# First modulation by halves of the features, shift from TensorE columns, context scale put off

## The chip, the core and the metric

The kernel runs on one core of one Trainium2 chip. Its engines run side by side, each through its own queue of instructions in order: TensorE (PE in the rows; PEld is its load of the stationary operand), VectorE (DVE), ScalarE (ACT), GpSimd (POOL) and SyncE (SP), which issues most of the DMAs. They wait for each other at semaphores. The metric is the device time of one execution in microseconds.

## What is computed

A backbone of two layers over 1024 latent tokens of width 1024, with 256 context tokens as a prefix. Each layer takes a root-mean-square norm, a modulation by a learned conditioning vector, a mixer and a mixture of 16 experts. The change is in what stands at the very start of layer 0:

```python
mod = sc_c @ w_mod[l] + b_mod[l]
sh1, scl1, g1, sh2, scl2, g2 = jnp.split(mod[:, None, :], 6, axis=-1)
h = _modulate(_rms(x, norm1[l]), sh1, scl1)        # h * (1 + scale) + shift
if need_c:
    modc = sc_ctx @ w_mod[l] + b_mod[l]
    csh1, cscl1, cg1, csh2, cscl2, cg2 = jnp.split(modc, 6)
    hc = _modulate(_rms(xc, norm1[l]), csh1, cscl1)
...
p = h @ w_in
q, k, v, gb, gc, xs = jnp.split(p, [K_OFF, V_OFF, B_OFF, C_OFF, X_OFF], axis=-1)
...
conv = gb * _short_conv(gc * xs, conv_w)
```

`sc_c` and `sc_ctx` are the conditioning vectors of latent and context after silu. Only the shift and the scale (2 x 1024 of the 6 x 1024 columns of `w_mod[0]`) are wanted before the first product of `h` with a weight. The context's own shift and scale are wanted much later, when the context's `hc` is made for keys and values.

## The kernel before

`layer0_mix` works with features on the partitions: a block of 512 tokens is held as 8 chunks (k = 0 to 7) of 128 features by 512 tokens. Every f32 operand of a product is split into a rounded part (`hi`) and the rest (`lo`), and a product is three matmuls per chunk (lines 385 to 387 in `fmm`): lo weight with hi data, hi with lo, hi with hi. The convolution runs in four groups of 128 channels (`cc`); for each group `conv_products` makes three projections (c, x, b) of both token blocks, that is 2 x 3 x 8 x 3 = 144 matmuls of 512 columns, each into its own bank of PSUM. `conv` then reads the banks (ACT copy in line 399 first).

What comes before the first product: `xn_tile` (four tiles of 128 tokens for block 0, one by one) loads a tile, squares and sums it on ACT, makes the reciprocal root in small steps on DVE (`rsqrt`), scales it on DVE, transposes it with 8 PE transposes (line 350) and copies it out of PSUM on ACT. `first_mods` loads rows of `w_mod` 128 at a time, shift and scale columns together (line 255). The shift is made on PE with the two vectors as the stationary operand and 512 columns of weights moving (line 257), copied to SBUF and turned by eight small transposes (line 279). The scale is accumulated on DVE, elementwise per partition, for latent and context (lines 261 and 263, 1024 wide), and summed over partitions by 16 matmuls of one column (line 269). Lines 283 to 286 add bias and norm for all 8 chunks at once. Then `modulate` makes hi and lo of all chunks: hi on ACT (line 361), lo in two steps (362, 363) on DVE, and for every fourth chunk on POOL.

`conv_weights(0)` loads the first group's three weights and splits them: the cast in line 164 on ACT, the subtraction in line 165 on DVE for c and on POOL for x and b. The tiles of block 1 are normalised between the products of block 0 by `more`. Behind that, `late_mods` accumulates the other modulation vectors on DVE (line 311), one step at a time, driven by `step`.

The code is written in program order; a scheduler with priorities decides in which order instructions stand in each engine's queue, and `mod(0)` is raised with `high_priority(400)`. An engine cannot pass an instruction that waits.

## Time and profile before

| | us |
|---|---|
| median of 3 runs | 2330.22 |
| lowest and highest | 2327.54, 2330.83 |
| profiled execution | 2327.57 |
| its span, first to last instruction | 2325.8 |
| PE busy in the span | 2144.5 (92%) |
| DVE busy | 1908.1 (82%) |
| ACT busy | 1398.4 (60%) |
| POOL busy | 650.5 (28%) |

The busy shares are of the whole span; the two mixtures of experts fill most of it. The change lies in the first 100 us, 4% of the span, so the stage has to be read by itself: which engine waits for which in it, and at what time it hands over to a stretch in which PE has no gaps. A row of the timeline merges equal instructions that follow each other; its first number is the start, the second the time from the first start to the last end. PE's matmuls overlap, so a pace is read from starts. The granted clock is a share of 2.4 GHz; the record has it at 1.00 from the start.

### The profile page before, as it was taken

To read this page: it belongs to the slowest core of one execution; us is meant where nothing else is said; L and a number is where in the kernel's file an instruction comes from. 1 tells how busy PE (TensorE), PEld (TensorE's weight loads), DVE (VectorE), ACT (ScalarE), POOL (GpSimd) and SP (SyncE) were. 2 spreads that over 40 slices of the span, in tenths; PEclk is the share of its full clock that TensorE was granted. 3 is DMA by queue.
4 is the path that set the end of the run, shared out by engine and by line. 5 is a ranking of instruction groups with operands and counts; after the bars stand their busy time and mean duration, and the time that the engine had idled before them with its cause. 6 is when DMAs were issued, how large, how long until landed. Compare 5 with 4: busy or idle time off the path is not lost.

```text
span 2325.8 us, 31653 instructions
## 1 busy us (share of the span) xinstructions
PE 2144.5 (92%) x10568; PEld 1740.9 (75%) x10568; DVE 1908.1 (82%) x2930; ACT 1398.4 (60%) x1864; POOL 650.5 (28%) x501
## 2 busy tenths in 40 slices
PE   7999989999985999999999699999859999999996
PEld 4787758988764788888888577777647888888884
DVE  7744577887498899999999756665989999999997
ACT  4413515777223788887887436233247888888874
POOL 1201101333442243242342220004313343342322
PEclk8999999999997999999999899999979999999998
DMA  8744552222847999999999502746579999999984
GB/s 289 214 118 141 182 203 73 82 73 103 323 173 282 354 363 376 371 369 375 362 370 367 167 28 67 262 165 213 205 277 343 379 369 360 380 374 357 374 316 154
DMA packets 187242, 602.03 MB, mean 259 GB/s; under 512 B 20557, under 2 KB 41790, under 8 KB 184004
## 3 DMA queue, kind: packets, MB, share of 16 engines
q1 hardware_dynamic: 168280, 533.38, 61.8%
q0 software_dynamic: 18800, 66.63, 9.6%
q8 instruction: 85, 1.39, 0.2%
q14 instruction: 77, 0.62, 0.1%
HBM read 545.89 MB, written 54.04 MB: 258 GB/s over the span
## 4 chain that ended last, share of the span: by engine, by line
PE 54%; DVE 17%; DMA 15%; issue 10%; ACT 3%; POOL 1%; SPq 0%; DVEq 0%; POOLq 0%; ACTq 0%
PE psum L1074 27%; DMA buf<-h2buf,buf 9%; DVE buf L165 3%; PE psum L654 3%; PE psum L1056 2%; DMA buf<-in_w_up_dram 2%; PE psum L1277 2%; PE psum L1278 2%; PE psum L1279 2%; PE psum L386 2%; PE psum L387 2%; PE psum L385 2%; PE psum L611 2%; DVE buf L185 2%; PE psum L612 1%
## 5 line engine op out<-in xcount | busy, mean ns | idle before, releaser
L165 DVE TENSOR_TENSOR buf<-buf,buf 128x1024 fp32r<-128x1024 f32 (+1 forms) x862 | 1025.3, 1235 | 87.2 <-ACT buf L164 71.5
L1074 PE MATMUL psum<-buf,buf 128*128 128x512 f32 x4608 | 1075.8, 392 | 2.7 <-ACT buf L1119 2.2
L164 ACT CAST buf<-buf 128x1024 fp32r<-128x1024 f32 (+1 forms) x868 | 876.1, 1020 | 324.4 <-PE psum L1074 153.9
L1074 PEld LDWEIGHTS psum<-buf,buf 128*128 128x128 f32 x4608 | 860.4, 188 | 180.9 <-ACT buf L1119 3.0
L1047 POOL DMA_INDIRECT buf<-h2buf,buf x32 | 230.9, 7215 | 598.2 <-DVE buf L1045 471.1
L386 PE MATMUL psum<-buf,buf 128*128 128x512 f32 (+1 forms) x352 | 135.5, 387 | 4.6 <-POOL buf L363 4.2
L385 PE MATMUL psum<-buf,buf 128*128 128x512 f32 (+1 forms) x352 | 134.1, 386 | 1.5 <-ACT buf L361 1.5
L387 PE MATMUL psum<-buf,buf 128*128 128x512 f32 (+1 forms) x352 | 134.4, 383 | 0.0
L164 ACT CAST buf<-psum 128x512 fp32r<-128x512 f32 (+1 forms) x153 | 88.8, 606 | 73.9 <-PE psum L1056 57.7
L311 DVE SCALAR_TENSOR_TENSOR buf<-buf,buf,buf 128x1024 f32<-128x1024 f32 x80 | 100.2, 1282 | 36.4 <-DMA buf<-in_w_mod_dram 33.5
L165 DVE TENSOR_TENSOR buf<-psum,buf 128x512 fp32r<-128x512 f32 (+1 forms) x153 | 105.2, 709 | 29.4 <-ACT buf L164 25.9
L1120 POOL TENSOR_TENSOR buf<-buf,buf 128x1024 f32<-128x1024 f32 x30 | 75.4, 2513 | 167.2 <-ACT buf L1119 167.2
L619 DVE TENSOR_REDUCE buf<-psum 128x1 f32<-128x1280 f32 x64 | 95.1, 1488 | 30.5 <-PE psum L612 23.4
L822 PE MATMUL psum<-buf,buf 128*128 128x512 f32 (+1 forms) x272 | 105.7, 391 | 0.0
L820 PE MATMUL psum<-buf,buf 128*128 128x512 f32 (+1 forms) x272 | 105.5, 389 | 0.0
L821 PE MATMUL psum<-buf,buf 128*128 128x512 f32 (+1 forms) x272 | 105.2, 388 | 0.0
L1277 PE MATMUL psum<-buf,buf 128*128 128x512 f32 x256 | 103.0, 403 | 1.3 <-DVE buf L165 1.3
L1278 PE MATMUL psum<-buf,buf 128*128 128x512 f32 x256 | 102.1, 399 | 0.0
L1279 PE MATMUL psum<-buf,buf 128*128 128x512 f32 x256 | 101.3, 396 | 0.0
L1056 PE MATMUL psum<-buf,buf 128*128 128x128 f32 x512 | 70.7, 283 | 28.3 <-DMA buf<-h2buf,buf 28.1
L1056 PEld LDWEIGHTS psum<-buf,buf 128*128 128x128 f32 x512 | 61.3, 145 | 40.7 <-DMA buf<-h2buf,buf 34.5
L835 ACT ACTIVATE buf<-buf 128x512 f32<-128x512 f32 (+1 forms) x34 | 20.6, 606 | 114.8 <-DVE buf L834 114.7
(272 smaller groups left out, 2958.5 us busy)
## 6 DMA issues: line engine op xcount, KB each, us to landing
buf<-in_w_gate_dram SPq DMA_DIRECT2D x256, 512.0 KB
buf<-in_w_up_dram SPq DMA_DIRECT2D x256, 512.0 KB
buf<-in_w_down_dram SPq DMA_DIRECT2D x256, 512.0 KB
buf<-in_w_mod_dram SPq DMA_DIRECT2D x80, 512.0 KB
buf<-xbuf SPq DMA_DIRECT2D x24, 512.0 KB
buf<-in_even_w_in_dram SPq DMA_DIRECT2D x20, 512.0 KB
buf<-in_x_dram SPq DMA_DIRECT2D x16, 512.0 KB
buf<-in_w_mod_dram SPq DMA_DIRECT2D x8, 1024.0 KB
```

The lines of the kernel that those rows point to most:

```text
L164: self.nc.scalar.copy(hi, src)
L165: (eng or self.nc.vector).tensor_tensor(out=lo, in0=src, in1=hi.bitcast(F32), op=OP.subtract)
L385: nc.tensor.matmul(out, wl[:, k, :], hh[:, k], start=(k == 0), stop=False)
L386: nc.tensor.matmul(out, wh[:, k, :], hl[:, k], start=False, stop=False)
L387: nc.tensor.matmul(out, wh[:, k, :], hh[:, k], start=False, stop=(k == KC - 1))
L822: nc.tensor.matmul(o, mh[:, k], wl[:, k, cs], start=False, stop=(k == KC - 1))
L1047: gather = nc.gpsimd.indirect_dma_start(out=xg.ap, out_offset=None, in_=self.H2, in_offset=bass.IndirectOffsetOnAxis(ap=idx.ap.bitcast(I32 ...
L1056: nc.tensor.transpose(b[:, j, :], src[:, k * P:(k + 1) * P], self.ident.ap)
L1074: mm = nc.tensor.matmul(self.bank(banks + n), st[:, k % 4], wt[:, n * 512:(n + 1) * 512], start=first, stop=last)
L1277: nc.tensor.matmul(b, hl[:, k], wh[:, k, :], start=(k == 0), stop=False)
L1278: nc.tensor.matmul(b, hh[:, k], wl[:, k, :], start=False, stop=False)
L1279: nc.tensor.matmul(b, hh[:, k], wh[:, k, :], start=False, stop=(k == KC - 1))
```

## The change

`w_mod` is loaded in two halves of the features. For each half there is a tile of shift weights and a tile of scale weights (8 chunks by 512 columns each, four DMAs a tile, `load_mods`). The loads of half 0, of the first group's convolution weights, of half 1 and of the second four x tiles are issued in this order.

The shift is no longer a row that is turned: the weights are the stationary operand, 128 x 128 at a time, and the two silu vectors are two moving columns (line 286, 32 matmuls for each half), so that it arrives with features on partitions. The scale is accumulated 512 wide, for the latent vector only (`weighted`, lines 262 and 264), and summed by four one-column matmuls (`to_scale`, line 271). The context's accumulation becomes a generator, `context_mods`, that is driven inside the loop over channel groups, nine steps a group.

`xn_group` normalises four tiles together: one chain of small DVE steps for four, transposes into two banks, copies of 512 on ACT. `modulate_rows` handles one chunk: for even chunks hi on ACT and lo in two DVE steps, for odd ones the scaling on ACT, hi by an ACT cast and lo in one DVE step. POOL no longer takes part in it. `conv_products` takes a range of chunks: the three projections of block 0 run over chunks 0 to 3, then, after the second half of the modulation, over chunks 4 to 7; block 1 follows whole. The raised priority is gone, as is `more`.

```diff
--- before.py
+++ after.py
@@ -245,46 +245,63 @@
         for b in (lam, pr, s2, e2):
             b.free()
 
-    def first_mods(self):
-
-        nc, A, a = self.nc, self.A, self.a
-        rows = self.PS[0:2, 4:6, :]
-        acc = A.alloc([2, D])
+    def load_mods(self, half):
+
+        tiles = []
+        for at, c in ((22528, 0), (30720, D)):
+            w = self.A.alloc([KC, 512], at=at + 4096 * half)
+            for i in range(0, KC, 2):
+                self.nc.sync.dma_start(w[:, i:i + 2], self.a["w_mod"][0, :, c + 512 * half:c + 512 * half + 512]
+                                       .rearrange("(k p) n -> p k n", p=P)[:, i:i + 2])
+            tiles.append(w)
+        return tiles
+
+    def weighted(self, acc, w, i, k):
+
+        if k == 0:
+            self.nc.vector.tensor_scalar(acc, w[:, k], self.sc[:, i, k:k + 1], None, op0=OP.mult)
+        else:
+            self.nc.vector.scalar_tensor_tensor(acc, w[:, k], self.sc[:, i, k:k + 1], acc, op0=OP.mult, op1=OP.add)
+
+    def to_scale(self, i, half, acc, out):
+
+        nc, A = self.nc, self.A
+        r = slice(4 * half, 4 * half + 4)
+        for j in range(4):
+            nc.tensor.matmul(out[:, j:j + 1], acc[:, j * P:(j + 1) * P], self.onec.ap, start=True, stop=True)
+        m = A.alloc([4])
+        nc.vector.tensor_tensor(out=m.ap, in0=out, in1=self.cols[:, 56 + 4 * half:60 + 4 * half], op=OP.add)
+        nc.vector.scalar_tensor_tensor(self.scale[:, i, r], m.ap, 1.0, self.cols[:, 16 + 4 * half:20 + 4 * half],
+                                       op0=OP.add, op1=OP.mult)
+        m.free()
+
+    def first_mods(self, half, tiles):
+
+        nc, A = self.nc, self.A
+        wsh, wsc = tiles
+        pc = self.bank(5 - 4 * half)[:, :8].rearrange("p (s j) -> p s j", s=2)
+        acc = A.alloc([512])
         for k in range(KC):
-            w = A.alloc([2 * D], zone="big")
-            nc.sync.dma_start(w.ap, a["w_mod"][0, k * P:(k + 1) * P, 0:2 * D])
-            for j in range(2):
-                nc.tensor.matmul(rows[:, j, :], self.sc[:, :, k], w[:, j * 512:(j + 1) * 512],
-                                 start=(k == 0), stop=(k == KC - 1))
-            for i in range(2):
-                if k == 0:
-                    nc.vector.tensor_scalar(acc[:, i], w[:, D:], self.sc[:, i, k:k + 1], None, op0=OP.mult)
-                else:
-                    nc.vector.scalar_tensor_tensor(acc[:, i], w[:, D:], self.sc[:, i, k:k + 1], acc[:, i],
-                                                   op0=OP.mult, op1=OP.add)
...
-        for j in range(2):
-            row = A.alloc([512])
-            if j % 2:
-                nc.scalar.copy(row[0:2, :], rows[:, j, :])
-            else:
-                nc.vector.tensor_copy(row[0:2, :], rows[:, j, :])
-            for i in range(4):
-                nc.tensor.transpose(pc[:, :, 4 * j + i], row[0:2, i * P:(i + 1) * P], self.ident[0:2, 0:2])
-            row.free()
-        self.shift, self.scale = A.alloc([2, KC], zone="const"), A.alloc([2, KC], zone="const")
-        both = lambda c: self.cols[:, None, c:c + 8].to_broadcast([P, 2, KC])
-        nc.vector.tensor_tensor(out=self.shift.ap, in0=pc[:, :, 0:8], in1=both(48), op=OP.add)
-        m = A.alloc([2, KC])
-        nc.vector.tensor_tensor(out=m.ap, in0=pc[:, :, 8:16], in1=both(56), op=OP.add)
-        nc.vector.scalar_tensor_tensor(self.scale.ap, m.ap, 1.0, both(16), op0=OP.add, op1=OP.mult)
-        m.free()
+        wsh.free()
+
+    def context_mods(self, tiles):
+
+        for half in range(2):
+            acc = self.A.alloc([512], at=30208)
+            for k in range(KC):
+                self.weighted(acc.ap, tiles[half][1], 1, k)
+                yield
+            self.to_scale(1, half, acc, self.bank(7)[:, 0:4])
+            acc.free()
+            tiles[half][1].free()
 
     def late_mods(self, passes):
 
@@ -352,6 +369,47 @@
         for b in (x, sq, st):
             b.free()
 
+    def xn_group(self, xs, dst):
+
+        nc, A = self.nc, self.A
+        junk, w = A.alloc([D]), A.alloc([4, 4])
+        ss, v, z, y = (w[:, i] for i in range(4))
+        for t, x in enumerate(xs):
+            nc.scalar.activation(junk.ap, x.ap, AF.Square, accum_out=ss[:, t:t + 1])
+        junk.free()
+        nc.vector.tensor_scalar(v, ss, 0.5 / D, 0.5 * EPS, op0=OP.mult, op1=OP.add)
...
+        for t, x in enumerate(xs):
+            nc.vector.tensor_scalar(x.ap, x.ap, y[:, t:t + 1], None, op0=OP.mult)
+            for g in range(2):
+                pt = self.bank(6 + g).rearrange("p (k n) -> p k n", n=P)
+                for k in range(4):
+                    nc.tensor.transpose(pt[:, k, :], x[:, (4 * g + k) * P:(4 * g + k + 1) * P], self.ident.ap)
+                nc.scalar.copy(dst[:, 4 * g:4 * g + 4, t * P:(t + 1) * P], pt)
+            x.free()
+        w.free()
+
+    def modulate_rows(self, b, k):
+
+        nc, A = self.nc, self.A
+        (hi, lo), xn = self.hT[b], self.xn_t[b]
+        hi, lo, xn, sc, sh = hi[:, k], lo[:, k], xn[:, k], self.scale[:, 0, k:k + 1], self.shift[:, 0, k:k + 1]
+        t = A.alloc([512])
+        if k % 2:
+            nc.scalar.activation(t.ap, xn, AF.Identity, bias=sh, scale=sc)
+            nc.scalar.copy(hi, t.ap)
+        else:
+            nc.scalar.activation(hi, xn, AF.Identity, bias=sh, scale=sc)
+            nc.vector.tensor_scalar(t.ap, xn, sc, sh, op0=OP.mult, op1=OP.add)
+        nc.vector.tensor_tensor(out=lo, in0=t.ap, in1=hi.bitcast(F32), op=OP.subtract)
+        t.free()
+
     def modulate(self, hi, lo, xn, scale, shift, n):
 
         nc, A = self.nc, self.A
@@ -377,21 +435,20 @@
         return {name: self.head_weights(off + cc * P, eng=self.nc.gpsimd if cc == 0 and name != "c" else None)
                 for name, off in (("c", 2048), ("x", 2560), ("b", 1536))}
 
-    def fmm(self, out, w, hT, mid=None):
+    def fmm(self, out, w, hT, ks=range(KC)):
 
         nc = self.nc
         (wh, wl), (hh, hl) = w[:2], hT
-        for k in range(KC):
+        for k in ks:
             nc.tensor.matmul(out, wl[:, k, :], hh[:, k], start=(k == 0), stop=False)
             nc.tensor.matmul(out, wh[:, k, :], hl[:, k], start=False, stop=False)
             nc.tensor.matmul(out, wh[:, k, :], hh[:, k], start=False, stop=(k == KC - 1))
-            if mid and k == KC // 2 - 1:
-                mid()
-
-    def conv_products(self, w, blk, step, mid=None):
+
+    def conv_products(self, w, blk, step=None, ks=range(KC)):
         for name, b in (("c", 0), ("x", 2), ("b", 4)):
-            self.fmm(self.bank(b + blk), w[name], self.hT[blk], mid)
-            step()
+            self.fmm(self.bank(b + blk), w[name], self.hT[blk], ks)
+            if step:
+                step()
 
     def conv(self, cc, w):
         nc, A = self.nc, self.A
@@ -491,28 +548,34 @@
         self.hT = [(A.alloc([KC, 512], F32R, at=4096 * b), A.alloc([KC, 512], F32R, at=8192 + 4096 * b))
                    for b in range(2)]
         self.cos, self.sin = A.alloc([SEQ], at=49152), A.alloc([SEQ], at=50176)
-        xn_t = [hl.alias([KC, 512], F32) for _, hl in self.hT]
-
-        def xn(t):
-            self.xn_tile(a["x"][0, t * P:(t + 1) * P, :], xn_t[t // 4][:, :, t % 4 * P:(t % 4 + 1) * P], 0 if t < 4 else 6)
-
-        def mod(b):
-            hh, hl = self.hT[b]
-            self.modulate(hh.ap, hl.ap, xn_t[b], self.scale[:, 0], self.shift[:, 0], 512)
-        for t in range(4):
-            xn(t)
-        self.first_mods()
-        A.zone["big"] = (16384, 30720)
+        self.xn_t = [hl.alias([KC, 512], F32) for _, hl in self.hT]
+        self.shift, self.scale = A.alloc([2, KC], zone="const"), A.alloc([2, KC], zone="const")
+
+        def load_x(b):
+            xs = [A.alloc([D]) for _ in range(4)]
+            for t, x in enumerate(xs):
+                nc.sync.dma_start(x.ap, a["x"][0, (4 * b + t) * P:(4 * b + t + 1) * P, :])
+            return xs
+        xs = load_x(0)
+        A.zone["big"] = (16384, 22528)
+        tiles = [self.load_mods(0)]
         w = self.conv_weights(0)
-        with self.tc.high_priority(400):
-            mod(0)
-        rest = list(range(4, NT))
-
-        def more():
-            if rest:
-                xn(rest.pop(0))
-        self.conv_products(w, 0, more, more)
-        mod(1)
+        tiles.append(self.load_mods(1))
+        self.xn_group(xs, self.xn_t[0])
+        self.first_mods(0, tiles[0])
+        for k in range(4):
+            self.modulate_rows(0, k)
+        self.conv_products(w, 0, ks=range(4))
+        self.first_mods(1, tiles[1])
+        xs = load_x(1)
+        for k in range(4, KC):
+            self.modulate_rows(0, k)
+        self.xn_group(xs, self.xn_t[1])
+        self.conv_products(w, 0, ks=range(4, KC))
+        for k in range(KC):
+            self.modulate_rows(1, k)
+        A.zone["big"] = (16384, 30208)
+        ctx_mods = self.context_mods(tiles)
         nc.sync.dma_start(self.cos.ap, a["rope_cos"])
         nc.sync.dma_start(self.sin.ap, a["rope_sin"])
         mods = self.late_mods(((0, 2 * D), (0, 4 * D), (1, 0)))
@@ -520,16 +583,20 @@
         def step(n):
             for _ in range(n):
                 next(mods, None)
-        vraw, vhi = A.alloc([KC, 512], at=30720), A.alloc([KC, 512], F32R, at=34816)
-        vlo = vraw.alias([KC, 512], F32R)
-        vw = vhi, vlo, vhi, vraw
         for cc in range(4):
             wn = self.conv_weights(cc + 1) if cc < 3 else None
             if cc:
                 self.conv_products(w, 0, lambda: step(1))
             self.conv_products(w, 1, lambda: step(1))
+            for _ in range(9):
+                next(ctx_mods, None)
             self.conv(cc, w)
             w = wn
+        for _ in ctx_mods:
+            pass
+        vraw, vhi = A.alloc([KC, 512], at=30720), A.alloc([KC, 512], F32R, at=34816)
+        vlo = vraw.alias([KC, 512], F32R)
+        vw = vhi, vlo, vhi, vraw
         A.zone["big"] = (25600, 30720)
         ch, cl = A.alloc([KC, CTX], F32R, at=16384), A.alloc([KC, CTX], F32R, at=18432)
         self.cT = ch, cl
```

PE, from the first use of `w_mod` to the first products. Before (257 is the shift as a row, 269 the scale's sums, 279 the turn of the shift, 385 to 387 are products):

```order
L257 MATMUL psum<-buf_258,buf_92 2x512 x2
L269 MATMUL psum<-buf_74,buf_215 128x1 x16
L279 MATMUL psum<-buf_66,buf_280 128x2 x4
L279 MATMUL psum<-buf_66,buf_286 128x2 x4
L385 MATMUL psum<-buf_107,buf_301 128x512
L385 MATMUL psum<-buf_107,buf_307 128x512
L386 MATMUL psum<-buf_108,buf_299 128x512
```

After, from the start (286 is the shift by columns, 393 are a tile's transposes, 271 the scale's sums, 443 to 445 are products, `buf_125` the shift weights of half 0):

```order
L286 MATMUL psum<-buf_92,buf_125 128x2 x16
L393 MATMUL psum<-buf_66,buf_117 128x128 x8
L286 MATMUL psum<-buf_92,buf_125 128x2 x8
L393 MATMUL psum<-buf_66,buf_118 128x128 x8
L286 MATMUL psum<-buf_92,buf_125 128x2 x8
L393 MATMUL psum<-buf_66,buf_119 128x128 x8
L393 MATMUL psum<-buf_66,buf_120 128x128 x8
L271 MATMUL psum<-buf_74,buf_225 128x1 x4
L443 MATMUL psum<-buf_107,buf_138 128x512
L444 MATMUL psum<-buf_108,buf_136 128x512
```

The column matmuls and the tiles' transposes alternate, and the scale's sums come behind both. Eight column matmuls of half 1 stand behind the sixth product.

PE, where the first half's products of block 0 end and the second half's begin (after; `buf_153` are the shift weights of half 1):

```order
L443 MATMUL psum<-buf_107,buf_150 128x512
L444 MATMUL psum<-buf_108,buf_148 128x512
L445 MATMUL psum<-buf_107,buf_148 128x512
L286 MATMUL psum<-buf_92,buf_153 128x2 x24
L271 MATMUL psum<-buf_74,buf_326 128x1 x4
L443 MATMUL psum<-buf_107,buf_138 128x512
```

The other 24 column matmuls of half 1 stand between the two halves of the products; before, nothing of the modulation stood among the products on PE.

DVE, where the last chunk of half 0 is made and half 1 is accumulated (after; 289 adds the bias to the shift and reads the column matmuls' bank, `buf_326` is the latent's accumulator of half 1, `buf_637` the context's of half 0):

```order
L410 TENSOR_TENSOR buf_108<-buf_286,buf_107 128x512
L262 TENSOR_SCALAR buf_326<-buf_158,buf_92 128x512
L264 SCALAR_TENSOR_TENSOR buf_326<-buf_158,buf_92,buf_326 128x512
L289 TENSOR_TENSOR buf_115<-psum,buf_90 128x2x4
L262 TENSOR_SCALAR buf_637<-buf_130,buf_92 128x512
L264 SCALAR_TENSOR_TENSOR buf_326<-buf_158,buf_92,buf_326 128x512
L264 SCALAR_TENSOR_TENSOR buf_637<-buf_130,buf_92,buf_637 128x512
```

The last two rows repeat to six of each, and then line 273 (bias of the scale) follows. The addition of the shift stands in front of most of the accumulation for the scale, and the context's steps between the latent's. Before, DVE held all accumulations in one piece, latent and context in turn, ahead of lines 283 to 286.

## Rows read from the trace of the kernel before

**Rows 1.** Busy time by stretch: PE, PEld, DVE, ACT, POOL; clock, DMA share, GB/s

```profile
0.00:10.00 10.00, 0.26 (x1) 0.26 (x2) 3.83 (x19) 2.64 (x4) 1.65 (x16) 1.00 0.52 174
10.00:20.00 10.00, 6.00 (x21) 3.58 (x21) 6.59 (x31) 6.80 (x11) 0.00 (x0) 1.00 1.01 426
...
90.00:100.00 10.00, 10.00 (x46) 8.28 (x45) 9.22 (x10) 5.63 (x8) 0.00 (x0) 1.00 0.98 243
...
170.00:180.00 10.00, 10.00 (x46) 8.29 (x45) 0.00 (x0) 1.01 (x1) 0.00 (x0) 1.00 0.00 0
```

**Rows 2.** Timeline of ACT: start, us, engine, line, operation, shapes, count, idle before

```profile
14.93 1.04 ACT L345 ACTIVATE buf<-buf 128x1024 f32<-128x1024 f32 x1
...
89.71 1.01 ACT L399 COPY buf<-psum 128x1024 f32<-128x1024 f32 x1 [3.17 <-PE psum L387]
```

**Rows 3.** Timeline of DVE in the opening

```profile
20.91 16.82 DVE L263 SCALAR_TENSOR_TENSOR buf<-buf,buf,buf 128x1024 f32<-128x1024 f32 x14
...
38.25 2.77 DVE L165 TENSOR_TENSOR buf<-buf,buf 128x1024 fp32r<-128x1024 f32 x1
```

**Rows 4.** Timeline of PE up to the first products

```profile
36.59 6.17 PE L269 MATMUL psum<-buf,buf 128*128 128x1 f32 x32 [1.43 <-DVE buf L263]
...
45.17 1.22 PE L385 MATMUL psum<-buf,buf 128*128 128x512 f32 x2 [1.47 <-ACT buf L361]
```

**Rows 5.** What PE waited for from 44 to 92: total, times, longest

```profile
PE psum L386 <- POOL buf L363: 4.2, 3, 2.6
```

**Rows 6.** Weight loads of line 269: timeline of two windows; min, median, max (ns)

```profile
36.59 0.97 PEld L269 LDWEIGHTS psum<-buf,buf 128*128 128x128 f32 x8 [2.36 <-DVE buf L263]
...
37.87 4.39 PEld L269 LDWEIGHTS psum<-buf,buf 128*128 128x128 f32 x20
...
L269 PEld LDWEIGHTS psum<-buf,buf x32: 186/333/333, 36.6 to 42.3; 128*128 128x128 f32 x32
```

**Rows 7.** Busy time by stretch as in rows 1, around the change of clock

```profile
37.00:38.00 1.00, 1.00 (x9) 1.00 (x8) 1.00 (x2) 0.48 (x1) 0.43 (x1) 0.76 1.07 415
...
51.00:52.00 1.00, 1.00 (x5) 0.83 (x4) 0.93 (x5) 0.98 (x4) 0.80 (x1) 0.91 0.80 315
```

**Rows 8.** Timeline of PE: the first and the fourth tile's eight transposes

```profile
10.01 1.92 PE L350 MATMUL psum<-buf,buf 128*128 128x128 f32 x8
...
22.82 1.09 PE L350 MATMUL psum<-buf,buf 128*128 128x128 f32 x8
```

**Rows 9.** Timeline of PE: products that follow each other

```profile
46.62 0.63 PE L387 MATMUL psum<-buf,buf 128*128 128x512 f32 x1
47.05 0.63 PE L386 MATMUL psum<-buf,buf 128*128 128x512 f32 x1
...
67.00 0.40 PE L385 MATMUL psum<-buf,buf 128*128 128x512 f32 x1
67.23 0.39 PE L386 MATMUL psum<-buf,buf 128*128 128x512 f32 x1
```

**Rows 10.** DVE accumulations by form: count, busy us, mean ns, idle before

```profile
L263 DVE SCALAR_TENSOR_TENSOR buf<-buf,buf,buf 128x1024 f32<-128x1024 f32 x14 | 16.8, 1277 | 0.0
...
L311 DVE SCALAR_TENSOR_TENSOR buf<-buf,buf,buf 128x1024 f32<-128x1024 f32 x80 | 100.2, 1282 | 36.4 <-DMA buf<-in_w_mod_dram 33.5 <-DMA buf<-in_b_mod_dram 2.7
...
L328 DVE SCALAR_TENSOR_TENSOR buf<-psum,buf 1x512 f32<-1x512 f32 x6 | 4.1, 676 | 4.0 <-PE psum L321 4.0
```

**Rows 11.** Modulation and splits: groups by form, and two single rows of DVE

```profile
L361 ACT ACTIVATE buf<-buf,buf,buf 128x512 fp32r<-128x512 f32 x16 | 13.1, 817 | 19.3 <-DVE buf L363 8.5 <-DVE buf L286 6.8 <-POOL buf L363 3.9
...
L362 DVE TENSOR_SCALAR buf<-buf,buf,buf 128x512 f32<-128x512 f32 x12 | 6.5, 544 | 2.4 <-POOL buf L363 1.9 <-ACT buf L351 0.4
...
L165 POOL TENSOR_TENSOR buf<-buf,buf 128x1024 fp32r<-128x1024 f32 x2 | 4.9, 2450 | 41.5 <-ACT buf L164 35.3 <-DMA buf<-in_x_dram 6.2
...
59.99 0.68 DVE L363 TENSOR_TENSOR buf<-buf,buf 128x512 fp32r<-128x512 f32 x1
...
60.67 1.22 DVE L165 TENSOR_TENSOR buf<-buf,buf 128x1024 fp32r<-128x1024 f32 x1
```

**Rows 12.** What DVE waited for from 180 to 330: total, times, longest

```profile
DVE buf L311 <- DMA buf<-in_w_mod_dram: 17.0, 6, 9.8
```

## What I expected before the run

> **What bounds the kernel now.** I read three views in this order: the busy table by stretches, the timeline of TensorE (PE), then those of DVE, ACT and POOL. The change touches only the first stage, so the question is when that stage hands over. Up to 90 us PE has idle slices; in 90:100 and in 170:180 it is busy for the whole stretch [rows 1]. The handover is the end of the first group's 144 products, which releases the ACT copy of line 399 at 89.71 [rows 2]. Behind that, PE runs in one piece for 80 us and more, so what the handover loses or gains goes on to the end nearly one to one: the expert weights start from places in the code that move along with it.
>
> Before the first product the chain is short. All 8.4 MB of the two modulation slices are loaded at some 426 GB/s [rows 1], the 14 big accumulations on DVE follow until 37.7 [rows 3], then 16 matmuls of one column each on PE take 36.59 to 42.76, the shift's eight small transposes follow, and the first product starts at 45.17 [rows 4]. Context rows cost half of the DVE chain. From 45 to 90 PE loses time to a half clock and to POOL's share of the modulation: 4.2 us in 3 waits [rows 5].
>
> **Three prices first.** (a) A matmul with a 128x128 f32 stationary tile and one or two columns is two hardware pieces. At full clock 8 weight loads of line 269 take 0.97 us, at half clock 20 take 4.39 [rows 6]; without the tail of the last one (0.19 and 0.33) the pitch is 0.11 and 0.213 us. One such matmul so costs 0.22 or 0.43 us. The granted clock fell to 0.76 in 37:38 while these ran, and was back (0.91) only in 51:52 [rows 7]: this work did not hold the full clock of 2.4 GHz, and the level after is 1.2 GHz. The shift's 2 columns have no row; this one-column row is the nearest, and the load of the weights sets both.
> (b) Eight transposes took 1.92 us at 10.01 and 1.09 at 22.82 [rows 8]. The record says 1.00 for both, but the first pace is that of the half clock. So PE starts slow and got fast somewhere between these two; what stood between them on PE beside such transposes were the 512-column matmuls of line 257. The changed opening has none of those, and I take it at half clock.
> (c) A product (512 columns) has a pitch of 0.23 at full clock (67.00 to 67.23) and 0.43 at half (46.62 to 47.05) [rows 9]. A 512-wide accumulation is estimated at 0.68 us from the one-partition row of that form [rows 10], which is also about half of 1.28; independent ones overlap by 0.08 (14 x 1.28 would be 17.9, the row shows 16.82 [rows 3, 10]), so 0.60 apart.
>
> The Trainium skill (TensorE: Matmul & The Clock Gate, Part 4: PE-mode transpose) says that transposes do not count as PE work for the clock gate. By that the interleaved transposes would not raise the clock either, which is what I take from the row; had they counted, the rival with the full clock would be the likelier.
>
> **Opening, after.** Bytes: x tiles 2.1 MB and the first piece of shift weights 0.5 MB. 1.7 MB have moved by 10 us (174 GB/s), the rest at 426 [rows 1]: about 12.1. Then the order of PE decides: 32 column matmuls and the transposes of the first two tiles stand in front of the last column matmul, 32 x 0.427 = 13.7 and 16 x 0.213 = 3.4, hence 29.2. (The tiles are scaled in time: the last square ended at 16.0 [rows 2], twelve small steps of 0.2 and one scaling of 0.75 follow, 19.1, and the first 16 column matmuls end at 18.9.) The shift's addition (line 289) stands on DVE *ahead of* the accumulations for the scale and waits for that last matmul, so the eight accumulations start at 29.3 although their weights landed before 22 (2.1 + 4.2 MB at 426 GB/s): 8 x 0.68 = 5.4, to 34.8. Four column matmuls 1.7, two tiny adds 0.4: 37.0. Then DVE does the first row's scaling (0.54) and one weight split (1.22 without POOL beside it) [rows 11]; the first product starts about 38.9, against 45.17 before. **Lead: 6.3 us.** The transposes removed (8 small ones, 1 us) and half of the 16.8 us of accumulation are in this lead; the loads no longer bound it.
>
> **Between the halves, after.** Three products, then x's weights: their low part is made on POOL, cast on ACT to 38.9, POOL 2.45 [rows 11]: 41.3. Three more, 42.6. Then 8 column matmuls of the second half stand in the way, 3.4: 46.0. Thirty products, ten at 0.43 and twenty at 0.23 (before, the clock was back at 51, six us after the first product [rows 4, 7]): 8.9, to 54.9. Now 24 column matmuls: a few at 0.22, then the clock falls as it did on line 269; 1 + 20 x 0.427 = 9.5, to 64.4. This is the step that costs. On DVE the second half's shift addition (line 289 again) stands after only two of its accumulations and waits for the 24, and *behind it* in the queue are six accumulations for the scale, interleaved with seven for the context, which nobody needs yet: 13 x 0.60 + 0.2 = 8.0, to 72.4. All this time PE has nothing. Four column matmuls 1.7, three small steps and one more context accumulation 1.0, ACT's 0.82 [rows 11]: the first product of the second half (k = 4) starts at 75.9.
>
> **Rest of the first group, after.** 36 products at 0.227 = 8.2, 32 transposes at 0.117 = 3.7, and some 2 for a half clock at the start: 89.8. Block 1: 72 x 0.227 = 16.3. Beside it DVE has 8 subtractions of 0.68, 4 scalings of 0.54, 7 context accumulations of 0.68, 6 gate accumulations of 1.28 and 2 splits of value weights of 0.68 [rows 10, 11], 21.5 in all and some 19.5 with overlap; that is 3 more than the products, and the last row's nine products follow it: 4 us of waiting. End: 110.1. What the change takes off POOL (4.2 us of PE's waits [rows 5]) is in this, since the new order has no such wait; without that it would be 114.
>
> Against 89.71 this is **+20.4 us**. Later steps: the three late vectors start later and the loads behind them (value weights, gates) are issued in another order; at 180 to 330 DVE waits for these loads (17.0 us in 6 times [rows 12]), which follow the progress of the stage. I put +0.6 there, with -4 to +5 as bounds. Sum on the profiled execution: 2327.6 + 21.0 = 2348.6. That execution lies 2.6 below the median of the runs, so the forecast is 2351.
>
> **Rivals.** *Full clock* (0.17): PE gets fast in the opening and column matmuls keep it so, at 0.22 each. The last of the opening's 32 is then out at 24.6 (16 of them and two tiles of 0.9 behind the first scaling at 19.1); 5.4, 0.9 and 0.4 bring 31.3, the first product comes at 33.2. The 30 products end about 45.5, the 24 matmuls at 50.9, 8.0 of DVE and 2.7 of small steps at 61.6, 11.9 and 20.3 more at 93.8; with some half clock left in it, 94 to 98. That is +4 to +8: 2336. For it: by 20 us the clock was full before. Against it: line 269 lost it [rows 7].
> *Heavier* (0.14): all products of the first half at half clock (+4), DVE slowed by POOL beside it for 2 (a split of 1.22 [rows 11] took 2.77 at 38.25 [rows 3]), block 1 bound by DVE for 3 more: 2360.
> *Columns cost nothing* (0.05), the one on the other side: the matmuls of two columns vanish beside the rest. Then the loads decide: scale weights landed at 22, tiles transposed by 27, first product near 28; the second half's weights are there at 35.5 (12.6 MB), its 15 accumulations on DVE end at 43, its products start at 45, and 13.9 and 20.3 later the group ends at 79: -10.5, 2319.5. From this to the forecast a piece goes from nothing to 0.213 us and the sum from -10.5 to +20.4; it turns at about 0.07.
> The Trainium skill (TensorE: Matmul & The Clock Gate, "Wait — 56ns, not 53.3ns?") puts the floor between matmuls at about 25 ns however few the columns, and that would make this last case true: 64 pieces in 1.6 us. The rows of line 269 with their 0.11 and 0.213 us a piece speak against it, and they decide here.
> *Nothing to see* (0.04): lead and loss cancel within the 0.2% that a measurement of this kernel can tell from no change (4.7 us): 2330.
>
> **Numbers.** Forecast 0.60 at 2351, its own range 2345 to 2356. Faster is the case of free columns, 0.05; within 0.2% the last one and a small part of the full clock, 0.06; slower the rest, 0.89. The range takes in most of the full clock and of the heavier case: 2337 to 2361.
>
> **What would show it.** In the profile after: line 286's weight loads about 0.21 apart in the opening; first product at 37 to 41; a clock near 0.5 again after the first 36 products; an idle stretch of PE of 6 to 9 us ended by DVE line 264, between the last of line 286 and line 271; the copy of line 456 at 105 to 116 in place of 89.71; and from there on the old timeline, shifted. It is wrong if line 286 runs at 0.05 or less, if the shift addition waits for nothing, or if 180:390 gives back ten us.

## The result: 28 us slower, and the profile after

The changed kernel takes 2356.79 us (median of four runs, 2353.71 to 2359.48) against 2328.88 for the kernel before in the same comparison: ratio 1.0118, 95% interval 1.0100 to 1.0137, or +27.9 us. The forecast was 2351, its range 2337 to 2361. The profiled execution took 2359.48 (span 2357.6); it is the slowest of the four, so the two traces differ by 31.8 us, some 4 more than the medians.

The first stage by stretches (us of the span; what follows are the busy times of PE, PEld, DVE, ACT and POOL, the granted clock, the share of the DMA engines, GB/s), to set beside [rows 1, 7]:

```profile
10.00:20.00 10.00, 6.28 (x30) 6.31 (x30) 4.71 (x16) 2.98 (x6) 0.00 (x0) 1.00 1.04 389
...
50.00:60.00 10.00, 10.00 (x51) 8.58 (x49) 1.57 (x3) 3.05 (x6) 0.00 (x0) 0.98 0.01 2
60.00:70.00 10.00, 5.67 (x27) 5.58 (x27) 4.25 (x8) 0.00 (x0) 0.00 (x0) 0.50 0.19 53
70.00:80.00 10.00, 4.33 (x14) 3.74 (x15) 7.79 (x20) 3.17 (x5) 0.00 (x0) 0.50 0.07 10
80.00:90.00 10.00, 10.00 (x51) 8.12 (x49) 7.89 (x15) 6.76 (x11) 0.00 (x0) 0.83 0.39 120
```

From 60 to 80 PE is busy half of the time and at the lower of its two levels (0.50, 1.2 GHz), while the loads have all but stopped (53 and 10 GB/s) and ACT is idle until 76.7: PE and DVE wait for each other there. PE's timeline shows the order; line 286 is the column matmuls, 271 the sum of the scale over partitions, 443 to 445 the products (before: [rows 4]). A row reads: start, length from the first start to the last end, engine, line, operation, shapes, count, and in brackets the idle time before it and what ended it.

```profile
13.72 6.96 PE L286 MATMUL psum<-buf,buf 128*128 128x2 f32 x32 [6.43 <-DMA buf<-in_w_mod_dram]
...
36.87 1.86 PE L271 MATMUL psum<-buf,buf 128*128 128x1 f32 x8 [2.56 <-DVE buf L264]
41.02 0.77 PE L443 MATMUL psum<-buf,buf 128*128 128x512 f32 x1 [2.29 <-ACT buf L164]
...
45.25 3.41 PE L286 MATMUL psum<-buf,buf 128*128 128x2 f32 x16
...
57.41 8.26 PE L286 MATMUL psum<-buf,buf 128*128 128x2 f32 x48
73.83 1.86 PE L271 MATMUL psum<-buf,buf 128*128 128x1 f32 x8 [8.16 <-DVE buf L264]
77.53 1.22 PE L443 MATMUL psum<-buf,buf 128*128 128x512 f32 x2 [1.83 <-ACT buf L408]
```

A count of 32 means 16 matmuls of two pieces each. The first product comes at 41.0 (before 45.2): a lead of 4.1 us. Then eight column matmuls stand among the products, 24 more follow them, and PE sits idle for 8.16 us. DVE tells why:

```profile
30.74 0.17 DVE L289 TENSOR_TENSOR buf<-psum,buf 128x8 f32<-128x8 f32 x1 [12.12 <-PE psum L286]
...
31.34 5.47 DVE L264 SCALAR_TENSOR_TENSOR buf<-buf,buf,buf 128x512 f32<-128x512 f32 x7
...
65.71 0.17 DVE L289 TENSOR_TENSOR buf<-psum,buf 128x8 f32<-128x8 f32 x1 [14.10 <-PE psum L286]
...
66.41 8.04 DVE L264 SCALAR_TENSOR_TENSOR buf<-buf,buf,buf 128x512 f32<-128x512 f32 x12
```

Twice the shift's addition (line 289) waits for the last column matmul, 12.12 and 14.10 us, and the accumulations for the scale run only behind it. The handover, ACT's first copy of the convolution, moved from 89.71 [rows 2] to 115.97:

```profile
115.97 1.01 ACT L456 COPY buf<-psum 128x1024 f32<-128x1024 f32 x1 [0.77 <-PE psum L445]
```

That is +26.3 of the 31.8 us between the two traces. The rest comes behind it: the first product of the attention scores starts at 402.8 against 372.5 (+30.3).

### The profile page after: what moved, and what is told of

Read it like the earlier page. It is cut to its first block, busy times and chain, and to the rows that moved or that the text cites. A ratio compares the mean times of both kernels' runs of the same rounds, so it can differ in the third digit from the quotient of the medians.

```text
span 2357.6 us, 31821 instructions
## 1 busy us (share of the span) xinstructions
PE 2159.9 (92%) x10656; PEld 1765.4 (75%) x10656; DVE 1905.6 (81%) x2904; ACT 1403.3 (60%) x1879; POOL 639.2 (27%) x493
## 4 chain that ended last, share of the span: by engine, by line
PE 45%; DMA 15%; DVE 15%; issue 11%; ACT 3%; POOL 0%; SPq 0%; DVEq 0%; POOLq 0%; ACTq 0%
PE psum L1141 23%; DMA buf<-h2buf,buf 10%; DVE buf L165 3%; PE psum L721 3%; PE psum L1123 2%; PE psum L1344 2%; PE psum L1345 2%; PE psum L678 2%; PE psum L1346 2%; DVE buf L185 2%; PE psum L679 1%; PE psum L712 1%; DVE buf L984 1%; DVE buf L901 1%; DMA buf<-in_w_gate_dram 1%
## 5 line engine op out<-in xcount | busy, mean ns | idle before, releaser
L165 DVE TENSOR_TENSOR buf<-buf,buf 128x1024 fp32r<-128x1024 f32 (+1 forms) x862 | 1022.8, 1231 | 78.8 <-ACT buf L164 64.5
L328 DVE SCALAR_TENSOR_TENSOR buf<-buf,buf,buf 128x1024 f32<-128x1024 f32 x80 | 100.2, 1279 | 36.8 <-DMA buf<-in_w_mod_dram 36.7
L165 DVE TENSOR_TENSOR buf<-psum,buf 128x512 fp32r<-128x512 f32 (+1 forms) x153 | 105.1, 708 | 27.9 <-ACT buf L164 24.3
```

The lines of the kernel that those rows point to most:

```text
L165: (eng or self.nc.vector).tensor_tensor(out=lo, in0=src, in1=hi.bitcast(F32), op=OP.subtract)
```

## Experiments

Theory A: column matmuls are slow (0.43 us a matmul at the lower clock) and DVE's addition holds the scale's accumulations up until they are done. Rivals: B, the columns alone are the loss; C, the halving itself (two passes of products, loads in another order) is. Theories D and E came from the first runs and are told where they arise. Each kernel is set against runs of the kernel before on the same chip (2328.5, 2330.2 and 2327.4 us in the three groups); "the copy" is ACT's first copy of the convolution.

### The columns alone, in the kernel before (e4_before_columns)

```diff
-            for j in range(2):
-                nc.tensor.matmul(rows[:, j, :], self.sc[:, :, k], w[:, j * 512:(j + 1) * 512],
-                                 start=(k == 0), stop=(k == KC - 1))
+            for j in range(8):
+                nc.tensor.matmul(pr[:, :, j], w[:, j * P:(j + 1) * P], self.sc[:, :, k],
+                                 start=(k == 0 and j == 0), stop=(k == KC - 1 and j == 7), skip_group_check=True)
...
-        nc.vector.tensor_tensor(out=self.shift.ap, in0=pc[:, :, 0:8], in1=both(48), op=OP.add)
+        nc.vector.tensor_tensor(out=self.shift.ap, in0=pr, in1=both(48), op=OP.add)
```

> The kernel before (2329 us; copy at 89.7) with one part of the change alone: the shift from 64 column matmuls of two columns in place of 16 matmuls of 512 moving columns with copies and eight small transposes. No halves, scale for both vectors as before. Theory A (half clock, 0.43 us each): 64 x 0.427 = 27.3 us behind the first weights at about 16, with 3.8 for transposes of the last two tiles and 6.2 for the 32 one-column matmuls of the scale behind them: 53 against 42.7; the turn of the row (2.4) goes; first product at 53 to 56 against 45.2, copy at 97 to 101, 2338, between 2334 and 2343. If columns run at full clock (0.22 each), 14 us hide behind the loads and DVE's accumulations and the turn of the row is won: 2327. Theory C (halving itself): 2327 to 2330.

Measured: 2342.48, 14.0 us above the kernel before (ratio 1.0060, 1.0044 to 1.0075); copy at 102.55. PE's timeline (257: columns, 269: the scale's one-column matmuls, 376: first product):

```profile
27.66 20.48 PE L257 MATMUL psum<-buf,buf 128*128 128x2 f32 x96
48.00 6.97 PE L269 MATMUL psum<-buf,buf 128*128 128x1 f32 x32
56.35 1.22 PE L376 MATMUL psum<-buf,buf 128*128 128x512 f32 x2 [1.39 <-ACT buf L352]
```

96 pieces in 20.48 us are 0.213 each, the price that was read off line 269 [rows 6]. First product (56.35) and copy come a little later than expected, the time is inside its range. So 14 us of loss need no halves. C alone is out, and so is the case in which columns cost nothing.

### The changed kernel with the shift as a row (e2_row)

```diff
-            for j in range(4):
-                nc.tensor.matmul(pc[:, :, j], wsh[:, k, j * P:(j + 1) * P], self.sc[:, :, k],
-                                 start=(k == 0 and j == 0), stop=(k == KC - 1 and j == 3), skip_group_check=True)
+            nc.tensor.matmul(out, self.sc[:, :, k], wsh[:, k], start=(k == 0), stop=(k == KC - 1))
...
+        nc.scalar.copy(row[0:2, :], out)
+        for j in range(4):
+            nc.tensor.transpose(pc[:, :, j], row[0:2, j * P:(j + 1) * P], self.ident[0:2, 0:2])
```

> The changed kernel with the shift made as a row again: for each half 8 matmuls with the two vectors stationary and 512 weight columns moving, an ACT copy and four small transposes, in place of 32 column matmuls. The addition still stands ahead of the accumulations on DVE. Theory A: 8 such matmuls take 3.4 us at full clock and 7 at half, against 13.7 for 32 columns; the first product comes some 8 us earlier than 41.0, the last columns between the halves (8.3 us) shrink to about 4 with the copy and the transposes, and PE's clock is full sooner: copy at 101 to 105, 2342, between 2336 and 2346. The accumulations then still wait for the shift, so PE's wait before the four one-column matmuls stays at 6 to 9 us between the halves. Theory C (halving itself): 2353 to 2357, since the halves and their loads are as they were.

Measured: 2333.22, ratio 1.0023 (1.0012 to 1.0033), 4.7 us above the kernel before: 23.2 of the 27.9 are gone. This is more than theory A gave; copy at 93.98. PE's timeline (286: the row matmuls, 271: the scale's sums, 447: products):

```profile
18.30 1.86 PE L286 MATMUL psum<-buf,buf 128*2 128x512 f32 x2
...
21.85 1.02 PE L286 MATMUL psum<-buf,buf 128*2 128x512 f32 x2
...
34.36 1.22 PE L447 MATMUL psum<-buf,buf 128*128 128x512 f32 x2 [2.58 <-ACT buf L412]
...
45.94 6.17 PE L286 MATMUL psum<-buf,buf 128*2 128x512 f32 x14
...
54.34 1.05 PE L271 MATMUL psum<-buf,buf 128*128 128x1 f32 x8 [1.16 <-DVE buf L293]
57.22 1.65 PE L447 MATMUL psum<-buf,buf 128*128 128x512 f32 x3 [1.83 <-ACT buf L412]
```

Two things were missing in the expectation. With 512 moving columns the clock was full by 21.85 (two pieces in 1.02 against 1.86 at 18.30), so the second half of the opening ran fast. And in this order DVE makes the second half's eight accumulations beside the last products and the row matmuls, ahead of the shift's addition (here line 293), so PE's wait before line 271 is 1.16, not 6 to 9:

```profile
42.48 5.48 DVE L264 SCALAR_TENSOR_TENSOR buf<-buf,buf,buf 128x512 f32<-128x512 f32 x7
...
54.12 0.16 DVE L293 TENSOR_TENSOR buf<-psum,buf 128x8 f32<-128x8 f32 x1
```

No line of the edit asks for that order; it came with it, so this run does not part the columns from the order. Together they had cost the columns' own time, the clock, and an order in which DVE could not work beside them.

### Only the addition moved (e1_shift_late)

```diff
-            self.weighted(acc.ap, wsc, 0, k)
-        nc.vector.tensor_tensor(out=self.shift[:, :, 4 * half:4 * half + 4], in0=pc,
...
+            last = self.weighted(acc.ap, wsc, 0, k)
+        with self.tc.issue_after(last.ins):
+            nc.vector.tensor_tensor(out=self.shift[:, :, 4 * half:4 * half + 4], in0=pc,
```

> The changed kernel (2356.8 us median; convolution copy at 116.0 in its profile) with one thing moved: the addition that finishes the shift stands on DVE behind the eight accumulations for the scale instead of ahead of them. Theory A (the column matmuls are slow AND the addition that waits for them holds the accumulations up): the accumulations run while PE does the columns. In the opening up to 5.5 us (7 accumulations in one piece) come off, between the halves up to 8.2 (PE's wait before line 271). Both together would be 13.7, 2343; part of it is used up where DVE meets other work, so 2347, between 2343 and 2351, and the copy at 102 to 110. Theory B (PE's columns alone are the loss, DVE would be late anyway): no more than 2 us, 2355 to 2357. Theory C (halving itself, two product passes with their loads, is the loss): also 2355 to 2357.

Measured: 2350.87, ratio 1.0100 (1.0081 to 1.0118), 22.4 us above the kernel before, 5.5 less than the changed kernel; copy at 111.62. The opening gained 3.1 us of the 5.5 at most (first product at 37.93 instead of 41.02); between the halves nothing was gained, PE again waited 7.86 us before line 271. So A's account of that wait was not the whole of it. DVE's timeline (262 and 264: accumulations, 290: the addition):

```profile
47.77 0.75 DVE L264 SCALAR_TENSOR_TENSOR buf<-buf,buf,buf 128x512 f32<-128x512 f32 x1
62.65 0.49 DVE L262 TENSOR_SCALAR buf<-buf,buf 128x512 f32<-128x512 f32 x1 [14.13 <-PE psum L286]
63.05 7.37 DVE L264 SCALAR_TENSOR_TENSOR buf<-buf,buf,buf 128x512 f32<-128x512 f32 x11
70.34 0.15 DVE L290 TENSOR_TENSOR buf<-psum,buf 128x8 f32<-128x8 f32 x1
```

What waits 14.13 us for the columns is now line 262, the *first accumulation of the context*. It reads nothing that PE makes. But its accumulator (at word 30208) lies inside the second half's shift weights (26624 to 30719), and it may not write before the last column matmul has read them. It stands between the second and third of the scale's accumulations, so the others stand behind it. In the changed kernel both waits were there, and the addition, ahead in the queue, hid the other. That is theory D.

### The accumulator at another place (e6_acc_moved, on top of e1_shift_late)

```diff
-            acc = self.A.alloc([512], at=30208)
+            acc = self.A.alloc([512], at=51776)
```

> The kernel of the run e1_shift_late with one number changed: the context's accumulator lies at a free place instead of inside the memory of the second half's shift weights. In e1_shift_late the context's first accumulation waited 14.1 us for the last column matmul (it may not write where weights are still read) and the second half's accumulations for the scale stood behind it on DVE. Theory D (this overlap is the second block): the accumulations now run while PE does the columns; PE's wait of 7.9 us before the second group of line 271 goes, the first product of the second half comes at 65 to 68 instead of 74.2, copy at 102 to 106 instead of 111.6, and the time falls by 6 to 9 against e1_shift_late, to 2342 to 2345. Rival (the second half's scale weights, or the columns themselves, are what is late): the wait stays at 5 or more and the time within 2 us of e1_shift_late (2351).

Measured: 2343.28, ratio 1.0062 (1.0044 to 1.0081), 13.1 us above the kernel before and so 9.3 less than e1_shift_late (7.6 between the two medians as they stand); copy at 103.3. PE's timeline:

```profile
54.94 6.58 PE L286 MATMUL psum<-buf,buf 128*128 128x2 f32 x48
61.38 1.84 PE L271 MATMUL psum<-buf,buf 128*128 128x1 f32 x8
64.52 1.65 PE L444 MATMUL psum<-buf,buf 128*128 128x512 f32 x3 [1.30 <-ACT buf L409]
```

Line 271 follows the columns without a pause, and the second half starts at 64.5 instead of 74.2. DVE's timeline and PE's row before the first product show that the new address changed more than this wait:

```profile
18.83 0.88 DVE L262 TENSOR_SCALAR buf<-buf,buf 128x512 f32<-128x512 f32 x2 [0.48 <-DMA buf<-in_w_mod_dram]
19.63 7.37 DVE L264 SCALAR_TENSOR_TENSOR buf<-buf,buf,buf 128x512 f32<-128x512 f32 x11
...
50.87 4.68 DVE L264 SCALAR_TENSOR_TENSOR buf<-buf,buf,buf 128x512 f32<-128x512 f32 x6
```

```profile
39.73 1.87 PE L271 MATMUL psum<-buf,buf 128*128 128x1 f32 x8 [5.63 <-DVE buf L264]
```

Two accumulators are begun in the opening, the latent's and the context's, where e1_shift_late begins one there. So the context's accumulations of half 0 no longer stand between the halves but before the first product, PE waits 5.63 us for DVE there, and the first product comes at 44.88 instead of 37.93. The rival of D is out: the second half's scale was accumulated by 55.5, while PE began the columns. D holds for the wait in e1_shift_late, and the idle stretch between the halves had two causes, one in the queue and one in the memory map; but what the address alone is worth is not shown, since seven steps of the context left the stretch with it and cost time in the opening. Net of that, order and address together are worth 14.8 us (27.9 less 13.1). That the 13.1 left are near what the columns cost alone (14.0) is therefore no check of the sum.

### Only the context's accumulations later (e3_ctx_late)

```diff
+                with self.tc.issue_after(self.done.ins):
+                    self.weighted(acc.ap, tiles[half][1], 1, k)
```

> The changed kernel with the context's 16 accumulations on DVE held back until the last subtraction of block 1 is done, so that none stands between the two halves. Theory A: seven of them come out of the piece of 13 between the halves (7 x 0.6 = 4.2 us) and up to 2.8 us of small waits in block 1 go: copy at 109 to 112, 2352, between 2349 and 2354; PE's wait before line 271 falls from 8.2 to about 4. If the context's work stands in the way only because the shift's addition holds it up (it would be free time otherwise), the same numbers hold here and the gain vanishes once the addition is moved. Theory C (halving itself): 2355 to 2357. If the later stage cannot place these accumulations, the copy is early and the end is not.

Measured: 2353.89, ratio 1.0115 (1.0096 to 1.0133). Against the changed kernel's ratio this is not resolved, though the rows did what was expected: PE's wait before line 271 is 4.86 instead of 8.16. The profiled execution, the fastest of six (2348.7 to 2360.4), has its copy at 106.9, 9.1 earlier, and 2.9 of that are no merit of the edit: here the 48 pieces between the halves ran at the full clock to the end, and it fell (0.72) as the last one ended. PE's timeline and the stretches (columns as above) on each side of the last piece:

```profile
56.95 5.41 PE L286 MATMUL psum<-buf,buf 128*128 128x2 f32 x48
...
61.00:62.00 1.00, 1.00 (x11) 1.00 (x11) 0.00 (x0) 0.00 (x0) 0.00 (x0) 1.00 0.00 0
62.00:63.00 1.00, 0.36 (x4) 0.28 (x3) 0.60 (x2) 0.00 (x0) 0.00 (x0) 0.72 0.00 0
```

In the changed kernel's trace the clock fell while the same pieces ran, and they took 8.26:

```profile
59.00:60.00 1.00, 1.00 (x10) 1.00 (x9) 0.00 (x0) 0.00 (x0) 0.00 (x0) 0.79 0.00 0
60.00:61.00 1.00, 1.00 (x6) 1.00 (x7) 0.00 (x0) 0.00 (x0) 0.00 (x0) 0.50 0.00 0
```

How much the median owes to the edit stays open.

### All three mended, halves kept (e5_all: e2_row, e1_shift_late and e3_ctx_late together)

> The changed kernel with three things mended: the shift as a row again (as in e2_row), the addition behind the accumulations, the context's accumulations behind block 1. Halves of the features stay. Theory A and D: against e2_row (copy at 94.0, 2333.2) nothing is left in front of the second half but 16 row matmuls and the turn: 1 to 2 us earlier there, and block 1 loses its waits for DVE (2.2 us): copy at 90 to 92, 2329 to 2332, the same as before (2328.5) within what can be told. What remains against before is 7 us of row matmuls between the halves and half-clock stretches after each pause. Theory C (halving itself loses more than that): 2333 and above.

Measured: 2328.93, ratio 0.9994 (0.9983 to 1.0006); copy at 87.85, earlier than expected. The second half's first product starts at 54.66 (e2_row 57.22):

```profile
54.66 1.65 PE L449 MATMUL psum<-buf,buf 128*128 128x512 f32 x3 [1.30 <-ACT buf L414]
```

Halves with the context's scale put off cost nothing that can be told, and they gain nothing either. C is out a second time.

### Only the context's scale put off, in the kernel before (e7_before_ctx)

```diff
-        acc = A.alloc([2, D])
+        acc = A.alloc([D])
+        wsc = self.wsc = A.alloc([KC, D], at=30720)
...
+            for _ in range(9):
+                next(ctx_mods, None)
             self.conv(cc, w)
```

> The kernel before with the other part of the change alone: the context's scale is accumulated late (behind the first subtractions of block 1, 16 accumulations of 512 between the channel groups), the latent's as before, 1024 wide, shift as a row, no halves. DVE's 16 accumulations before the first product become 8, and so the loads decide: the last weights land at about 34.5, the last accumulation ends near 36 instead of 37.7, 8 column matmuls in place of 16 take 3 instead of 6.2: first product at 40.5 to 42.5 instead of 45.2, copy at 86 to 88 instead of 89.7, 2325.5, between 2324 and 2328. If the 16 accumulations cost as much later as they save now (DVE is 82% busy over the span): 2328 to 2331.

Measured: 2329.18, ratio 1.0005 (0.9990 to 1.0020); first product at 42.13, copy at 89.9. The 3.0 us of lead were there and did not arrive at the copy. DVE and PE show where they went (385 and 386: modulation, 411: product):

```profile
42.67 2.47 DVE L385 TENSOR_SCALAR buf<-buf,buf,buf 128x512 f32<-128x512 f32 x1
...
45.24 2.66 DVE L386 TENSOR_TENSOR buf<-buf,buf 128x512 fp32r<-128x512 f32 x1
...
78.09 0.60 PE L411 MATMUL psum<-buf,buf 128*128 128x512 f32 x1 [2.55 <-POOL buf L386]
```

Beside POOL's splits of the first weights (42.18 to 47.4) these two DVE steps take 2.47 and 2.66 us instead of 0.55 and 0.69. An earlier start moved them into that stretch. Theory E is that POOL so gave the lead back.

### POOL taken out of the stage (e8_ctx_nopool on e7_before_ctx, e9_all_nopool on e5_all)

```diff
-            eng = nc.gpsimd if k % 4 == 3 else nc.vector
...
...
-        return {name: self.head_weights(off + cc * P, eng=self.nc.gpsimd if cc == 0 and name != "c" else None)
+        return {name: self.head_weights(off + cc * P, eng=None)
```

Both kernels split all first weights on DVE; e8_ctx_nopool also makes the low part of every chunk there and, as the changed kernel does, scales the odd chunks on ACT.

> The kernel of the run e7_before_ctx without POOL in this stage: the low parts of every fourth chunk go to DVE (odd chunks scaled on ACT, as in the changed kernel), and the splits of the first x and b weights too. In e7_before_ctx the first product came 3.0 us earlier than before (42.1 against 45.2) and the copy did not (89.9 against 89.7): PE's waits for POOL lines 165 and 386 (1.0, 2.6 and 0.5 us) and two DVE operations of 2.5 and 2.7 us beside POOL in place of 0.55 and 0.7. Theory E (POOL gave the lead back): first product at 41 to 42.5, copy at 85 to 87.5, and a time 2 to 4 us under the kernel before. Rival (DVE takes POOL's place as the bound of block 0 and 1): copy at 88.5 to 91 and a time within 2 us of it.

> The kernel of the run e5_all with the splits of the first x and b weights on DVE instead of POOL. In e5_all an addition of four columns took 1.39 us and a subtraction 1.59 beside POOL in place of 0.16 and 0.69, on the path to the first products: 2.1 us. Theory E: copy at 85 to 87.5 instead of 87.8, and a time 1 to 2 us under e5_all, thus 2 to 3 under the kernel before, if the later stage is as in e5_all. Rival: DVE has 2.4 us of splits more in the opening, the copy stays at 87.5 to 88.5, and the time with it.

Measured: e8_ctx_nopool has its copy at 83.43, 6.3 us before the kernel before, more than theory E gave, and takes 2326.30, ratio 0.9995 (0.9985 to 1.0006). e9_all_nopool has its copy at 87.8, as its rival had it, and takes 2327.90, ratio 1.0000 (0.9988 to 1.0011). So with POOL out of the stage the lead arrives at the copy in the one and not in the other. In e8_ctx_nopool three things went together (the splits, the low parts, the scaling on ACT), and which of them brought it is not shown. In neither does the total differ from the kernel before by what can be told. No version here beats it.

### Where a lead or a loss goes behind the stage

In the profiled executions, in us:

| kernel | copy | first scores | from one to the other |
|---|---|---|---|
| before | 89.7 | 372.5 | 282.8 |
| after | 116.0 | 402.8 | 286.8 |
| e1_shift_late | 111.6 | 397.2 | 285.6 |
| e2_row | 94.0 | 374.8 | 280.8 |
| e3_ctx_late | 106.9 | 392.8 | 285.9 |
| e4_before_columns | 102.6 | 388.8 | 286.2 |
| e5_all | 87.8 | 373.0 | 285.2 |
| e6_acc_moved | 103.3 | 388.7 | 285.4 |
| e7_before_ctx | 89.9 | 378.5 | 288.6 |
| e8_ctx_nopool | 83.4 | 370.8 | 287.4 |
| e9_all_nopool | 87.8 | 371.3 | 283.5 |

The stretch behind the handover takes 280.8 to 288.6 us, in one execution each, and that follows none of the parts: e4_before_columns has neither halves nor a late context and shows 286.2, e5_all and e7_before_ctx have the late context with 285.2 and 288.6. In the changed kernel one pause that can be named is the first context tile (line 367), at which PE waits 6.07 us (before 3.17) and the clock falls. Rows of PE after and before, of ACT, and of the stretch:

```profile
268.85 1.94 PE L367 MATMUL psum<-buf,buf 128*128 128x128 f32 x8 [6.07 <-issue]
```

```profile
240.59 1.06 PE L350 MATMUL psum<-buf,buf 128*128 128x128 f32 x8 [3.17 <-ACT buf L164]
```

```profile
262.35 0.62 ACT L501 CAST buf<-buf 64x512 fp32r<-64x512 f32 x1 [8.68 <-DVE buf L486]
...
264.90 1.06 ACT L362 ACTIVATE buf<-buf 128x1024 f32<-128x1024 f32 x1
```

```profile
260.00:280.00 20.00, 13.93 (x54) 11.30 (x53) 14.50 (x36) 10.28 (x17) 1.19 (x1) 0.83 0.30 100
```

The tile's square (line 362) stands on ACT behind casts that wait 8.68 us for DVE's rotation. This pause does go along with a part: it is 6.0 to 6.1 us in all four traces that have halves and columns (after, e1_shift_late, e3_ctx_late, e6_acc_moved), 4.4 in e4_before_columns, and 3.2 to 3.6 in the six in which the shift is a row. Whether the columns themselves or the late handover behind them makes DVE late there was not tried and stays open.

## Why the prediction was right, and where its terms were off

The direction was right, and so was the mechanism but for half the cause of one wait; the size came out 5.8 us low, inside the range. Part of that closeness is luck: the sum was made for the profiled execution, and there it was 10.9 low (2348.6 against 2359.5). Step by step, times of the trace after beside those of the sum:

| step | forecast | measured |
|---|---|---|
| first column matmul | 12.1 | 13.7 |
| shift's addition | 29.2 | 30.7 |
| accumulations done | 34.8 | 36.8 |
| first product | 38.9 | 41.0 |
| 24 columns | 54.9 to 64.4 | 57.4 to 65.7 |
| 13 accumulations behind them | 8.0 | 8.7 |
| first product of the second half | 75.9 | 77.5 |
| the second half's products done | 89.8 | 92.5 |
| copy | 110.1 | 116.0 |
| first scores, against before | +21.0 | +30.3 |

Of the 9.3 us between +21.0 and +30.3, 5.9 are in the rows up to the copy and 3.4 behind it; the medians lie 4 us nearer to each other than the traces.

- *The price of a column matmul* was right. Line 286's weight loads in the trace after:

```profile
L286 PEld LDWEIGHTS psum<-buf,buf x128: 188/333/338, 13.7 to 65.3; 128*128 128x128 f32 x128
```

  The median of 333 ns is the half-clock value of [rows 6], and from the first column to the addition 17.0 us went by where the sum had 17.1. The full clock's price is measured too: 48 pieces in 5.41 us in e3_ctx_late, 0.113 each. Between the halves the clock fell later than the sum had it, and the 24 columns took 8.3 instead of 9.5. The Trainium skill (TensorE: Matmul & The Clock Gate, LDWEIGHTS (loading the stationary operand)) puts a load at its columns divided by 1.2, in ns, from which 107 for 128 columns is an estimate. The 113 at the full clock are near it, and the 213 at the half are twice as much.
- *The opening's clock* was right: without 512-column matmuls it stayed at half. e2_row is the other side of it, where the row matmuls brought the full clock by 21.85. The rival with the full clock is out.
- *The start* was mis-sized by 1.6 us. The second 10 us moved 389 GB/s, not 426, but by the sum's own bytes that makes only 0.2. By 13.7 some 3.1 MB had moved (172 GB/s to 10 us, 379 from there), where the sum had 2.6 in front of the first column; so more than those bytes went ahead of it or beside it. Which is not shown.
- *A 512-wide accumulation* was mis-sized: the one-partition row of [rows 10] gave 0.68, the full width takes 0.743 and 0.67 apart (12 in 8.04). On 8 in the opening and 13 between the halves this makes some 1.2.
- *The wait between the halves* had the right place and size (8.16 us, named as 6 to 9) and half of its cause. The sum put it on the addition alone; e1_shift_late showed a second block, the context's accumulator in the memory of the weights, and with it elsewhere the wait is gone (e6_acc_moved). Whoever had mended only what the prediction named would have kept the wait.
- *The second half and block 1*, from 77.5 to 116.0, took 38.5 where the sum had 34.2: the second half 15.0 instead of 13.9, block 1 up to the copy 23.4 instead of 20.3. A term was forgotten: `to_scale` for the context issues eight matmuls of line 271, and they stand among block 1's products:

```profile
92.12 0.40 PE L445 MATMUL psum<-buf,buf 128*128 128x512 f32 x1
92.73 0.96 PE L443 MATMUL psum<-buf,buf 128*128 128x512 f32 x3 [0.21 <-ACT buf L408]
93.53 0.95 PE L271 MATMUL psum<-buf,buf 128*128 128x1 f32 x8
...
102.43 0.98 PE L271 MATMUL psum<-buf,buf 128*128 128x1 f32 x8
```

  That is 1.9 us. (The row at 92.12 is the 36th product of the second half, the one at 92.73 the first of block 1.) PE's waits for DVE in block 1 are 3.1 in 6 times, near the 4 of the sum; the rest of block 1's excess is not taken apart.
- *The later stage* was taken at +0.6 with -4 to +5 around it, and took +4.0 from the copy to the first scores: inside its bounds, at their upper end. Of that, 2.9 are in the longer pause at the context's tile (above); the rest stays open.
- The *heavier* rival came out nearest in time (2360) but not by its mechanism: the 30 products took 8.9 us as in the forecast, and block 1 waited less for DVE, not more; only DVE beside POOL was there (line 410, 2.77 us at 43.85).

How the 27.9 us split: 23.2 go with the columns and the order that came with them (e2_row), the rest with the two orders (e5_all). Taken the other way round, order and address give 14.8 with the columns still in place (e6_acc_moved), so the parts overlap: the columns are dear by themselves (14.0 us in e4_before_columns) and dearer where a queue stands behind them.

## What to carry to other kernels

Price a matmul by its stationary load as well as by its columns: turning a product round, so that 128x128 weights are loaded for two moving columns, saves a transpose and pays 0.22 us at the full clock or 0.43 at the half for each load. When an instruction is held by a wait, look at everything behind it in its queue, and before moving it ask what would wait next: a buffer that overlaps one still being read waits just as a true dependence does, and is hidden behind the first. A lead at the start of a program counts only as far as it is still there at the end of the stage, and then at the next stage's end: 6.3 us at the copy left about 1 in the total, which can't be told from none.

## What the hardware showed that was not expected

- The same 48 small pieces kept the full clock to the end in one trace (5.41 us in e3_ctx_late) and lost it on the way in others (6.58 in e6_acc_moved, 8.26 in the changed kernel, granted 0.79 in 59:60), in nearly the same instruction order on PE. A term of 3 us in the sum hung on it. Each is one execution of another kernel, so whether the program decides it is not shown.
- A step on DVE beside POOL can be held until POOL's instruction ends, even a very small one: in e2_row the scale's last step, over four columns,

```profile
32.01 1.39 DVE L274 SCALAR_TENSOR_TENSOR buf<-buf,buf 128x4 f32<-128x4 f32 x1
```

  took 1.39 us instead of 0.16 (line 274 in e6_acc_moved and in the changed kernel: 0.15 or 0.16). The Trainium skill (SBUF — State Buffer, Who interferes with whom) says that such an instruction, with two inputs in SBUF, contends with one of POOL that reads there; the trace agrees: POOL's split of 1024 columns ran beside it from 31.05 to 33.39, and the step ended as that did.
